# A decoder layer on one core: VectorE's order in the up-projection, and the pace of a gather's row fetches

## The chip, the cores and the metric

The kernel runs on one core of a Trainium2 chip. The metric is the device time of one execution in microseconds (us), lower being better. A core has five engines with an instruction queue each: TensorE (PE, with its weight loads as PEld), VectorE (DVE), ScalarE (ACT), GpSimd (POOL) and SyncE (SP), which here only issues transfers. ScalarE and GpSimd issue transfers too; all of them run on the core's 16 DMA engines.

## The reference

One decoder layer over 512 tokens of width 1024 in float32: token mixing (mLSTM heads and sliding-window attention), cross-attention into 256 memory tokens, then PEER, a retrieval over 128 x 128 single-neuron experts, and a final RMSNorm. The change lies in PEER, which per token is

```
qh = (xb @ w_pq).reshape(T, P_HEADS, 2, P_KEY_DIM)
v1, i1 = lax.top_k(s1, P_TOPK)          # s1, s2: scores against the two sets of 128 keys
v2, i2 = lax.top_k(s2, P_TOPK)
top_s, pos = lax.top_k(cand_s, P_TOPK)  # 16 of the 16 x 16 sums, for each of 8 heads
eidx = jnp.take_along_axis(cand_i, pos, axis=-1)
g = jax.nn.softmax(top_s, axis=-1)
u = expert_down[eidx]
a = jax.nn.gelu(jnp.einsum('thkd,td->thk', u, xb), approximate=False)
coef = g * a
out = jnp.einsum('thk,thkd->td', coef, expert_up[eidx])
```

So every token uses 8 x 16 = 128 experts, each with a row of 1024 in expert_down and one in expert_up.

## The kernel before

The 512 tokens are four blocks of 128 (NB = 4). PEER is done in two ways.

**Block 0 by gathering** (NG = 1). `gather` is a Python generator that issues one row step at a time. Step j < 128 fetches, for each of the 128 tokens, its j-th expert's row of expert_down (an indirect DMA on POOL's queue, 128 rows of 4 KB, into one of eight buffers "rows"), and VectorE multiplies it with the token and sums it into `dots` (L773). Then the coefficients are made, and steps 128 to 255 fetch rows of expert_up, which VectorE adds into `gacc` (L783). That is 256 row steps.

**Blocks 1 to 3 densely** (ND = 3, TD = 384 tokens). All 128 x 128 experts are treated as 128 tiles of 128 experts. A *down tile* (class `Down`) loads its weights in pairs (`draw`, GRP = 2), ScalarE casts them to dh, VectorE makes the remainder dl = draw − dh (L828), and TensorE computes 8 x 3 = 24 matmuls of 384 columns into acc_d (L839 to L841), which ScalarE puts through GELU. An *up tile* (`up_tile`) reads the gates `wt` of four tiles at a time from the DRAM tensor `wd`, the rows `uraw` of expert_up for two tiles at a time, and where the GELU output was spilled (72 of the tiles, SP) reads it back as `gsr`; VectorE multiplies it with the gates (cf, L898), ScalarE casts cf to ch and uraw to uh, VectorE makes the remainders cl (L901) and ul, called lo in the code (L891), and TensorE does 3 blocks x 2 halves x 3 = 18 matmuls of 512 columns into six PSUM banks acc_u (L912 to L914). uh, ul, ch and cl have two buffers each, so that the operands of tile u need those of tile u−2 to be done with.

**Stages around the change.** `gating` builds the dense gates of blocks 2 and 3 in 32 steps q each: one-hot tiles, eight matmuls per two groups into `w` (L745), ScalarE copies them to `stg` (two buffers), and after each eight steps a transfer of 2 MB writes stg to wd on ScalarE's queue. Between the steps, early down tiles fill TensorE. In block 3 the first 12 row steps of the gather are consumed at the steps q of GQ (9, 11, ... 31). Then come LEAD = 7 down tiles, the *lead*, with ten more row steps (GLD), and then the up-projection loop: 128 up tiles in the order of `up_order`, with the remaining 49 down tiles made ahead in it (`ahead`, `made_by`) and the remaining 256 − 22 row steps dealt out over tiles 0 to 119 (GST) by `rows`. The matmuls of the last two up tiles are ordered by block, so that `finish` (residual, final RMSNorm and the output) can begin by block; block 0 is finished from gacc.

**What sets the order.** The program is written in one order, and a planner (the Tile framework, with a timeline of its own) makes each engine's instruction order from the dependences and the written order as priority; the order on an engine is then fixed. `tc.issue_after(x)` keeps what is written in it behind x on x's own engine, in order of issue alone. In the loop before, VectorE's order is the planner's; each row step is only kept behind c.cf or c.cl of its tile. The row numbers come from `c.eidx`; row steps after the first 22 read a copy of it, `c.rowid`, which VectorE writes behind the last lead tile's dl (L1209).

Of the kernel before, what the change touches and what calls it, by code (L numbers as in the profile page):

```python
# [11 lines left out]
F32 = mybir.dt.float32  # L12
# [9 lines left out]
P = 128  # L22
# [29 lines left out]
GLD = 10  # L52
GST = 120
WST, WTL = 3, 5

# [643 lines left out]
def gating(c, early, ga):  # L699
# [3 lines left out]
    for b in range(NG + NS, NB):  # L703
# [29 lines left out]
        for q in range(32):  # L733
# [17 lines left out]
            with c.tc.issue_after(mm.ins):  # L751
                early.fill(FGT)
            if b == NB - 1 and q in GQ:
                with c.tc.issue_after(c.sc[HD - 1][-1].ins), c.tc.issue_after(last.ins):
                    step(ga, 1)


def gather(c):
# [6 lines left out]
    def fetch(src, j):  # L765
        r = gp.tile([P, D], F32, tag="rows", bufs=8, name="rows")
        G.indirect_dma_start(out=r, out_offset=None, in_=src,  # L767
                             in_offset=bass.IndirectOffsetOnAxis(ap=c.rowid[:, j:j + 1], axis=0))
        return r

    for j in range(P):
        r = fetch(c.a["down_r"], j)
        V.tensor_tensor_reduce(r, r, c.xn0, 1.0, 0.0, op0=ALU.mult, op1=ALU.add, accum_out=dots[:, j:j + 1])  # L773
        yield
# [3 lines left out]
    for j in range(P):  # L778
        r = fetch(c.a["up"], j)
        if j == 0:  # L780
            V.tensor_scalar(c.gacc, r, coef[:, j:j + 1], None, op0=ALU.mult)
        else:
            V.scalar_tensor_tensor(c.gacc, r, coef[:, j:j + 1], c.gacc, op0=ALU.mult, op1=ALU.add)  # L783
        yield


# [30 lines left out]
class Down:  # L817


    def __init__(self, c, i2):  # L820
        nc, dp = c.nc, c.dp
        self.c, self.i2 = c, i2
        if i2 % GRP == 0:
            c.draw = dp.tile([P, GRP, D], F32, tag="draw", bufs=2, name="draw")
            nc.sync.dma_start(c.draw, c.a["down_t"][i2 // GRP])
        raw = c.draw[:, i2 % GRP]
# [39 lines left out]

def up_tile(c, u, i2, gel, acc):
    nc, up = c.nc, c.up
    V, A, T = nc.vector, nc.scalar, nc.tensor
    if i2 % UG == 0:  # L870
        c.wt = up.tile([P, ND, UG * P], F32, tag="wt", bufs=2, name="wt")
        for b in range(ND):
            i = nc.sync.dma_start(c.wt[:, b], c.wd[b][i2 // UG])
            for j in c.sc[HD - 1] if b == 0 else ():
                c.tc.add_manual_dep(i.ins, j.ins.name, SYNC, reason="gates complete")
# [3 lines left out]
    if i2 % GRP == 0:  # L879
        c.uraw = up.tile([P, GRP, D], F32, tag="uraw", bufs=3, name="uraw")  # L880
        nc.sync.dma_start(c.uraw, c.a["up"].rearrange("(i p) d -> p i d", p=P)[:, i2:i2 + GRP])
    g = c.gsr[:, i2 % UG] if i2 < SP else gel[i2]
    raw = c.uraw[:, i2 % GRP]
    last = u == NK - 1
    if last:
        z = c.xlo.rearrange("p k t -> p (k t)")
        hi, lo = z[:, 0:D], z[:, D:2 * D]
        A.copy(hi, raw)
    else:
        hi, lo = split3(c, up, raw, "u", 2)  # L890
    V.tensor_tensor(lo, raw, f32(hi), op=ALU.subtract)  # L891
    cf = up.tile([P, TD], F32, tag="cf", bufs=2, name="cf")
    if last:
        ch, cl = z[:, 2 * D:2 * D + TD], z[:, 3 * D:3 * D + TD]
    else:
        ch = up.tile([P, TD], F32R, tag="ch", bufs=2, name="ch")
        cl = up.tile([P, TD], F32R, tag="cl", bufs=2, name="cl")
    c.cf = V.tensor_tensor(cf.rearrange("p (b t) -> p b t", t=32), g.rearrange("p (b t) -> p b t", t=32),  # L898
                    c.wt.rearrange("p b (q i t) -> p (b q) i t", q=4, i=UG)[:, :, i2 % UG], op=ALU.mult)
    A.copy(ch, cf)  # L900
    c.cl = V.tensor_tensor(cl, cf, f32(ch), op=ALU.subtract)  # L901
    return hi, lo, ch, cl
# [230 lines left out]
def body(tc, a, out, dbg=None):  # L1133
# [3 lines left out]
    with ExitStack() as st:  # L1137
# [57 lines left out]
        with pool("gather", side="right") as c.gp:  # L1195
            c.rowid = c.eidx
# [4 lines left out]
            assert len(gel) == SP  # L1201

            for n in range(LEAD):
                ahead(1)
                with tc.issue_after(c.dl.ins):
                    step(ga, GLD * (n + 1) // LEAD - GLD * n // LEAD)
            c.rowid = c.gp.tile([P, P], I32, name="rowid")
            with tc.issue_after(c.dl.ins):
                nc.vector.tensor_copy(c.rowid, c.eidx)  # L1209
            pst_ = [c.ps.tile([P, 512], F32, tag=t, name="acc_u") for t in "bbbbaa"]  # L1210
            acc = [[pst_[2 * b], pst_[2 * b + 1]] for b in range(ND)]
            last, mms = [], []
            g0 = len(GQ) + GLD
# [105 lines left out]
```

## Time and profile before

| | |
|---|---|
| median of 3 runs | 1648.53 us (1648.18 to 1648.61) |
| the profiled execution, its own time | 1650.35 us |
| its span, first to last instruction | 1648.7 us |
| TensorE busy | 1605.7 us (97%) |
| VectorE busy | 1233.7 us (75%) |
| ScalarE busy | 723.2 us (44%) |
| GpSimd busy | 590.8 us (36%) |

Times in the rows are us from the start of the span unless ns is named. Matmuls overlap in TensorE's pipeline and their ends are modelled, so the sum of their durations is more than the time from one start to the next. L912 is line 912 of the kernel before.

### The profile page before, as it was taken

To read this page: it belongs to the slowest core of one execution; us is meant where nothing else is said; L and a number is where in the kernel's file an instruction comes from. 1 tells how busy PE (TensorE), PEld (TensorE's weight loads), DVE (VectorE), ACT (ScalarE), POOL (GpSimd) and SP (SyncE) were. 2 spreads that over 40 slices of the span, in tenths; PEclk is the share of its full clock that TensorE was granted. 3 is DMA by queue.
4 is the path that set the end of the run, shared out by engine and by line. 5 is a ranking of instruction groups with operands and counts; after the bars stand their busy time and mean duration, and the time that the engine had idled before them with its cause. 6 is when DMAs were issued, how large, how long until landed. Compare 5 with 4: busy or idle time off the path is not lost.

```text
span 1648.7 us, 23081 instructions
## 1 busy us (share of the span) xinstructions
PE 1605.7 (97%) x8387; PEld 1411.7 (86%) x8388; DVE 1233.7 (75%) x2704; ACT 723.2 (44%) x1217; POOL 590.8 (36%) x427
## 2 busy tenths in 40 slices
PE   8998999999999999999999999999999999999994
PEld 5775698888999999999998888888888888888883
DVE  5366564564877887777787888787888888878898
ACT  5464444443544444578664333333333333333332
POOL 2000000000027787878121543443433444333451
PEclk9999999999999999999999999999999999999997
DMA  5227144232254435668999999999989999988895
GB/s 214 77 97 287 54 151 154 77 153 106 97 187 126 116 75 138 196 178 234 321 312 342 410 391 346 344 338 339 345 320 366 339 327 333 359 319 313 328 364 180
DMA packets 151122, 402.17 MB, mean 244 GB/s; under 512 B 28368, under 2 KB 62304, under 8 KB 138848
## 3 DMA queue, kind: packets, MB, share of 16 engines
q1 hardware_dynamic: 58208, 240.04, 39.4%
q0 software_dynamic: 55360, 134.32, 24.8%
q10 hardware_dynamic: 37440, 26.35, 5.1%
q8 instruction: 66, 1.08, 0.3%
q14 instruction: 48, 0.39, 0.1%
HBM read 357.07 MB, written 43.58 MB: 243 GB/s over the span
## 4 chain that ended last, share of the span: by engine, by line
PE 89%; DVE 4%; DMA 3%; ACT 1%; issue 1%; POOL 0%; DVEq 0%; SPq 0%; POOLq 0%; ACTq 0%
PE acc_u L912 10%; PE acc_u L913 10%; PE acc_u L914 10%; PE acc_d L841 10%; PE acc_d L839 10%; PE acc_d L840 10%; PE acc_f L1013 4%; PE acc_f L1015 4%; PE acc_f L1014 4%; PE w L745 3%; DMA wd<-stg 3%; PE acc_t L1026 2%; PE acc_t L1028 2%; PE acc_t L1027 2%; DVE gacc L783 1%
## 5 line engine op out<-in xcount | busy, mean ns | idle before, releaser
L839 PE MATMUL acc_d<-xhi,dh 128*128 128x384 f32 x1024 | 349.9, 342 | 1.1 <-ACT gsp L861 1.0
L841 PE MATMUL acc_d<-xhi,dl 128*128 128x384 f32 x1024 | 345.1, 337 | 1.7 <-DVE dl L828 1.7
L840 PE MATMUL acc_d<-xlo,dh 128*128 128x384 f32 x1024 | 343.7, 336 | 0.0
L913 PE MATMUL acc_u<-ul,ch 128*128 128x512 f32 x762 | 297.8, 391 | 0.0
L914 PE MATMUL acc_u<-uh,cl 128*128 128x512 f32 x762 | 296.7, 391 | 0.0
L690 POOL DMA_INDIRECT wd<-gg,ei x128 | 229.9, 1796 | 147.4 <-DVE ei L684 84.8
L912 PE MATMUL acc_u<-uh,ch 128*128 128x512 f32 x762 | 264.4, 390 | 0.1
L767 POOL DMA_INDIRECT rows<-in_up_dram,rowid x128 | 169.2, 1322 | 236.9 <-DVE gacc L783 209.0
L828 DVE TENSOR_TENSOR dl<-draw,dh 128x1024 fp32r<-128x1024 f32 x128 | 156.1, 1220 | 93.2 <-ACT dh L790 93.1
L900 ACT CAST ch<-cf 128x384 fp32r<-128x384 f32 x127 | 65.1, 514 | 356.6 <-issue 339.4
L790 ACT CAST dh<-draw 128x1024 fp32r<-128x1024 f32 x128 | 134.0, 1049 | 195.3 <-PE acc_d L840 179.4
L767 POOL DMA_INDIRECT rows<-in_down_r_dram,rowid x106 | 142.5, 1344 | 199.4 <-DVE dots L773 159.2
L839 PEld LDWEIGHTS acc_d<-xhi,dh 128*128 128x128 f32 x1024 | 192.9, 188 | 5.5 <-ACT gsp L861 1.3
L840 PEld LDWEIGHTS acc_d<-xlo,dh 128*128 128x128 f32 x1024 | 192.9, 188 | 3.7
L841 PEld LDWEIGHTS acc_d<-xhi,dl 128*128 128x128 f32 x1024 | 192.7, 188 | 4.0 <-DVE dl L828 2.6
L914 PEld LDWEIGHTS acc_u<-uh,cl 128*128 128x128 f32 x762 | 143.0, 188 | 29.4
L913 PEld LDWEIGHTS acc_u<-ul,ch 128*128 128x128 f32 x762 | 143.0, 188 | 28.7
L912 PEld LDWEIGHTS acc_u<-uh,ch 128*128 128x128 f32 x762 | 142.9, 188 | 28.3 <-ACT ch L900 0.5
L891 DVE TENSOR_TENSOR ul<-uraw,uh 128x1024 fp32r<-128x1024 f32 x127 | 154.8, 1220 | 12.4 <-ACT uh L790 11.9
L783 DVE SCALAR_TENSOR_TENSOR gacc<-rows,coef,gacc 128x1024 f32<-128x1024 f32 x127 | 162.6, 1280 | 0.9
L773 DVE CUSTOM_DVE_ANT_0 rows<-rows,xn 128x1024 f32<-128x1024 f32 x128 | 153.7, 1218 | 0.0
L901 DVE TENSOR_TENSOR cl<-cf,ch 128x384 fp32r<-128x384 f32 x127 | 70.7, 557 | 86.6 <-ACT ch L900 86.2
(344 smaller groups left out, 2644.7 us busy)
## 6 DMA issues: line engine op xcount, KB each, us to landing
draw<-in_down_t_dram SPq DMA_DIRECT2D x64, 1024.0 KB, 6.6
uraw<-in_up_dram SPq DMA_DIRECT2D x64, 1024.0 KB, 9.0
wt<-wd SPq DMA_DIRECT2D x96, 256.0 KB, 9.7
wd<-stg ACTq DMA_DIRECT2D x8, 2048.0 KB, 17.4
gd<-gsp SPq DMA_DIRECT2D x18, 768.0 KB, 3.9
gsr<-gd SPq DMA_DIRECT2D x18, 768.0 KB, 9.9
wd<-zero ACTq DMA_DIRECT2D x1, 8192.0 KB, 26.9
raw<-in_w_pq_dram SPq DMA_DIRECT2D x8, 1024.0 KB, 4.9
```

Of the source, the lines that this page charges most:

```text
L690: i = G.indirect_dma_start(out=out, out_offset=bass.IndirectOffsetOnAxis(ap=ei[:, h, k:k + 1], axis=0), in_=c.gg[:, NG, hh, k:k + 1], in_o ...
L767: G.indirect_dma_start(out=r, out_offset=None, in_=src, in_offset=bass.IndirectOffsetOnAxis(ap=c.rowid[:, j:j + 1], axis=0))
L773: V.tensor_tensor_reduce(r, r, c.xn0, 1.0, 0.0, op0=ALU.mult, op1=ALU.add, accum_out=dots[:, j:j + 1])
L783: V.scalar_tensor_tensor(c.gacc, r, coef[:, j:j + 1], c.gacc, op0=ALU.mult, op1=ALU.add)
L828: c.dl = nc.vector.tensor_tensor(self.lo, raw, f32(self.hi), op=ALU.subtract)
L839: T.matmul(acc[:, :TD], self.hi[:, ks], c.xhi[:, k, NG * P:], start=(k == 0), stop=False)
L840: T.matmul(acc[:, :TD], self.hi[:, ks], c.xlo[:, k, NG * P:], start=False, stop=False)
L841: T.matmul(acc[:, :TD], self.lo[:, ks], c.xhi[:, k, NG * P:], start=False, stop=(k == KT - 1))
L891: V.tensor_tensor(lo, raw, f32(hi), op=ALU.subtract)
L912: T.matmul(acc[b][n], ch[:, t], hi[:, d], start=st, stop=False)
L913: T.matmul(acc[b][n], ch[:, t], lo[:, d], start=False, stop=False)
L914: c.mm = T.matmul(acc[b][n], cl[:, t], hi[:, d], start=False, stop=sp)
```

## The change

Four things are changed, all in PEER.

1. From the first up tile to the last row step VectorE's instructions keep the written order (`tc.manual_schedule` for VectorE alone). The written order of a step u is now: half of the step's rows (rounded up), then lo and cl of tile u, the dl of down tiles made in the step, the other rows, and cf of tile u+1. For this `up_tile` is split: `up_gates` does the loads and cf one tile ahead.
2. The row numbers of the first 22 row steps are copied column by column into `c.rid` by VectorE (`row_number`), at every odd step q of the last gating block and once in each lead tile; a fetch reads its column there.
3. The copy of all row numbers, `c.rowid`, moves from behind the seventh lead tile to the fifth.
4. Gate reads (wt) and up loads (uraw) are kept behind the last lead tile's load (`c.lead`) on SyncE's queue.

```
+GI = range(1, 32, 2)
...
+            if b == NB - 1 and q in GI:
+                with c.tc.issue_after(last.ins):
+                    row_number(c)
...
         G.indirect_dma_start(out=r, out_offset=None, in_=src,
-                             in_offset=bass.IndirectOffsetOnAxis(ap=c.rowid[:, j:j + 1], axis=0))
+                             in_offset=bass.IndirectOffsetOnAxis(
+                                 ap=(c.rid if src is c.a["down_r"] and j < len(GQ) + GLD else c.rowid)[:, j:j + 1], axis=0))
...
+def row_number(c):
+
+    n = c.nid
+    if n < len(GQ) + GLD:
+        c.nc.vector.tensor_copy(c.rid[:, n:n + 1], c.eidx[:, n:n + 1])
+        c.nid += 1
...
-def up_tile(c, u, i2, gel, acc):
+def up_gates(c, u, i2, gel):
+
     nc, up = c.nc, c.up
-    V, A, T = nc.vector, nc.scalar, nc.tensor
     if i2 % UG == 0:
         c.wt = up.tile([P, ND, UG * P], F32, tag="wt", bufs=2, name="wt")
         for b in range(ND):
-            i = nc.sync.dma_start(c.wt[:, b], c.wd[b][i2 // UG])
+            with c.tc.issue_after(c.lead.ins):
+                i = nc.sync.dma_start(c.wt[:, b], c.wd[b][i2 // UG])
...
     if i2 % GRP == 0:
         c.uraw = up.tile([P, GRP, D], F32, tag="uraw", bufs=3, name="uraw")
-        nc.sync.dma_start(c.uraw, c.a["up"].rearrange("(i p) d -> p i d", p=P)[:, i2:i2 + GRP])
+        with c.tc.issue_after(c.lead.ins):
+            nc.sync.dma_start(c.uraw, c.a["up"].rearrange("(i p) d -> p i d", p=P)[:, i2:i2 + GRP])
     g = c.gsr[:, i2 % UG] if i2 < SP else gel[i2]
...
+    c.raw = c.uraw[:, i2 % GRP]
+    c.gated = up.tile([P, TD], F32, tag="cf", bufs=2, name="cf")
+    nc.vector.tensor_tensor(c.gated.rearrange("p (b t) -> p b t", t=32), g.rearrange("p (b t) -> p b t", t=32),
+                            c.wt.rearrange("p b (q i t) -> p (b q) i t", q=4, i=UG)[:, :, i2 % UG], op=ALU.mult)
+
+
+def up_tile(c, u):
...
+    V.tensor_tensor(lo, raw, f32(hi), op=ALU.subtract)
     A.copy(ch, cf)
-    c.cl = V.tensor_tensor(cl, cf, f32(ch), op=ALU.subtract)
+    V.tensor_tensor(cl, cf, f32(ch), op=ALU.subtract)
     return hi, lo, ch, cl
...
             for n in range(LEAD):
                 ahead(1)
                 with tc.issue_after(c.dl.ins):
+                    row_number(c)
+                    if n == LEAD - 3:
+                        c.rowid = c.gp.tile([P, P], I32, name="rowid")
+                        nc.vector.tensor_copy(c.rowid, c.eidx)
                     step(ga, GLD * (n + 1) // LEAD - GLD * n // LEAD)
-            c.rowid = c.gp.tile([P, P], I32, name="rowid")
-            with tc.issue_after(c.dl.ins):
-                nc.vector.tensor_copy(c.rowid, c.eidx)
+            assert c.nid == g0
+            c.lead = c.draw_dma
...
-            for u, i2 in enumerate(up_order()):
+            order = up_order()
+            dve = ExitStack()
+            dve.enter_context(tc.manual_schedule(engines={mybir.EngineType.DVE}))
+            up_gates(c, 0, order[0], gel)
+            for u, i2 in enumerate(order):
+                n = rows[u + 1] - rows[u]
+                step(ga, n - n // 2)
+                parts = up_tile(c, u)
                 if u >= FREE:
                     with tc.issue_after(mms[u - FREE].ins):
                         ahead(made_by(u) - len(gel))
                 else:
                     ahead(made_by(u) - len(gel))
-                parts = up_tile(c, u, i2, gel, acc)
-                for i in range(rows[u + 1] - rows[u]):
-                    with tc.issue_after((c.cf if i == 0 else c.cl).ins):
-                        step(ga, 1)
+                step(ga, n // 2)
+                if u < NK - 1:
+                    up_gates(c, u + 1, order[u + 1], gel)
...
             step(ga, 2 * P)
+            dve.close()
```

## Rows read from the trace of the kernel before

**Rows 1.** The page: span, and busy time of each engine.

```profile
span 1648.7 us, 23081 instructions
...
PE 1605.7 (97%) x8387; PEld 1411.7 (86%) x8388; DVE 1233.7 (75%) x2704; ACT 723.2 (44%) x1217; POOL 590.8 (36%) x427
```

**Rows 2.** The chain that ended last, from 1606 us: start, length, work.

```profile
1606.84 1.36 PE acc_u L912 x6
...
1610.92 1.33 PE acc_u L912 x6
...
1636.61 0.58 POOL frst L943
...
1642.42 1.32 DVE hb L931 x2
```

**Rows 3.** Stretches: length; each engine's busy time, instructions; granted clock; DMA share; GB/s.

```profile
892.00:1000.00 108.00, 108.00 (x521) 95.02 (x522) 89.05 (x132) 39.02 (x54) 49.61 (x38) 1.00 1.01 395
...
1620.00:1628.00 8.00, 7.24 (x32) 5.64 (x31) 7.86 (x7) 0.00 (x0) 0.76 (x1) 1.00 0.89 303
1628.00:1649.00 21.00, 0.00 (x0) 0.00 (x0) 14.37 (x27) 5.12 (x16) 2.16 (x4) 0.53 0.33 128
```

**Rows 4.** VectorE by line, 892 to 1627: count, busy us, mean ns, idle before.

```profile
L783 DVE SCALAR_TENSOR_TENSOR gacc<-rows,coef,gacc 128x1024 f32<-128x1024 f32 x124 | 158.7, 1280 | 0.8
L891 DVE TENSOR_TENSOR ul<-uraw,uh 128x1024 fp32r<-128x1024 f32 x126 | 153.7, 1219 | 10.9 <-ACT uh L790 10.3 <-DMA uraw<-in_up_dram 0.4
...
L901 DVE TENSOR_TENSOR cl<-cf,ch 128x384 fp32r<-128x384 f32 x127 | 70.7, 557 | 86.6 <-ACT ch L900 86.2
L828 DVE TENSOR_TENSOR dl<-draw,dh 128x1024 fp32r<-128x1024 f32 x50 | 61.1, 1222 | 24.2 <-ACT dh L790 24.2
```

**Rows 5.** Line L783 alone from 1594 us: count, ns min/median/max, starts.

```profile
L783 DVE SCALAR_TENSOR_TENSOR gacc<-rows,coef,gacc x18: 1271/1279/1285, 1593.1 to 1630.1; 128x1024 f32<-128x1024 f32 x18
```

**Rows 6.** Last gating block: stretches as in rows 3, ScalarE, gate writes' landing, POOL.

```profile
810.00:814.00 4.00, 1.89 (x13) 1.70 (x12) 2.58 (x7) 3.97 (x10) 0.00 (x0) 0.95 1.05 386
814.00:818.00 4.00, 4.00 (x20) 4.00 (x19) 2.89 (x8) 0.79 (x3) 1.15 (x1) 0.62 0.99 353
818.00:822.00 4.00, 4.00 (x29) 4.00 (x28) 2.60 (x8) 3.84 (x9) 0.00 (x0) 1.00 0.33 119
...
807.06 1.08 ACT L747 COPY stg<-w 128x512 f32<-128x512 f32 x2 [4.44 <-DMA wd<-stg]
...
DMA to landing us min/median/max: 12.2/17.4/27.0
...
774.71 1.13 POOL L767 DMA_INDIRECT rows<-in_down_r_dram,eidx  x1 [0.30 <-issue]
```

**Rows 7.** Final norm in order of time, VectorE and ScalarE.

```profile
1635.71 0.15 DVE L927 TENSOR_TENSOR frst<-fss 128x1 f32<-128x1 f32 x1
...
1635.78 0.68 DVE L925 TENSOR_TENSOR hb<-hb,acc_u 128x512 f32<-128x512 f32 x1
1635.85 0.58 ACT L926 ACTIVATE acc_u<-hb 128x512 f32<-128x512 f32 x1
```

**Rows 8.** ScalarE's casts for one up tile, in order of time.

```profile
1602.61 0.51 ACT L900 CAST ch<-cf 128x384 fp32r<-128x384 f32 x1 [2.61 <-issue]
1603.03 1.04 ACT L790 CAST uh<-uraw 128x1024 fp32r<-128x1024 f32 x1
```

**Rows 9.** Around the first up tile: SyncE, ScalarE, POOL, in order of time.

```profile
884.40 0.95 SPq L881 DMA_DIRECT2D uraw<-in_up_dram  x2
...
889.46 2.00 ACT L790 CAST uh<-uraw 128x1024 fp32r<-128x1024 f32 x2 [1.31 <-DMA uraw<-in_up_dram]
...
899.57 1.67 POOL L767 DMA_INDIRECT rows<-in_down_r_dram,rowid  x1 [26.81 <-DVE rowid L1209]
```

**Rows 10.** Row fetches, 900 to 930, then 1000 to 1600: median to landing.

```profile
rows<-in_down_r_dram,rowid POOLq DMA_INDIRECT x16, 14.6
...
rows<-in_down_r_dram,rowid POOLq DMA_INDIRECT x69, 7.2
```

More of the change, by code (lines that the diff above doesn't have):

```diff
@@ L772, in gather @@
         r = fetch(c.a["down_r"], j)
-        V.tensor_tensor_reduce(r, r, c.xn0, 1.0, 0.0, op0=ALU.mult, op1=ALU.add, accum_out=dots[:, j:j + 1])
+        c.row = V.tensor_tensor_reduce(r, r, c.xn0, 1.0, 0.0, op0=ALU.mult, op1=ALU.add, accum_out=dots[:, j:j + 1])
         yield
@@ L782, in gather @@
         else:
-            V.scalar_tensor_tensor(c.gacc, r, coef[:, j:j + 1], c.gacc, op0=ALU.mult, op1=ALU.add)
+            c.row = V.scalar_tensor_tensor(c.gacc, r, coef[:, j:j + 1], c.gacc, op0=ALU.mult, op1=ALU.add)
         yield
+def row_number(c):
[3 more added lines that the diff above has]
+        c.nid += 1
 def split3(c, pool, raw, tag, bufs):
@@ L824, in __init__ @@
             c.draw = dp.tile([P, GRP, D], F32, tag="draw", bufs=2, name="draw")
-            nc.sync.dma_start(c.draw, c.a["down_t"][i2 // GRP])
+            c.draw_dma = nc.sync.dma_start(c.draw, c.a["down_t"][i2 // GRP])
         raw = c.draw[:, i2 % GRP]
@@ L880, in up_tile @@
         c.uraw = up.tile([P, GRP, D], F32, tag="uraw", bufs=3, name="uraw")
-        nc.sync.dma_start(c.uraw, c.a["up"].rearrange("(i p) d -> p i d", p=P)[:, i2:i2 + GRP])
+        with c.tc.issue_after(c.lead.ins):
+            nc.sync.dma_start(c.uraw, c.a["up"].rearrange("(i p) d -> p i d", p=P)[:, i2:i2 + GRP])
     g = c.gsr[:, i2 % UG] if i2 < SP else gel[i2]
-    raw = c.uraw[:, i2 % GRP]
-    last = u == NK - 1
-    if last:
+    c.raw = c.uraw[:, i2 % GRP]
[3 more added lines that the diff above has]
+def up_tile(c, u):
+    nc, up = c.nc, c.up
+    V, A = nc.vector, nc.scalar
+    raw, cf = c.raw, c.gated
+    if u == NK - 1:
         z = c.xlo.rearrange("p k t -> p (k t)")
         hi, lo = z[:, 0:D], z[:, D:2 * D]
+        ch, cl = z[:, 2 * D:2 * D + TD], z[:, 3 * D:3 * D + TD]
         A.copy(hi, raw)
@@ L890, in up_tile @@
         hi, lo = split3(c, up, raw, "u", 2)
[L891 to L895, printed above, removed]
         ch = up.tile([P, TD], F32R, tag="ch", bufs=2, name="ch")
         cl = up.tile([P, TD], F32R, tag="cl", bufs=2, name="cl")
-    c.cf = V.tensor_tensor(cf.rearrange("p (b t) -> p b t", t=32), g.rearrange("p (b t) -> p b t", t=32),
-                    c.wt.rearrange("p b (q i t) -> p (b q) i t", q=4, i=UG)[:, :, i2 % UG], op=ALU.mult)
+    V.tensor_tensor(lo, raw, f32(hi), op=ALU.subtract)
     A.copy(ch, cf)
-    c.cl = V.tensor_tensor(cl, cf, f32(ch), op=ALU.subtract)
+    V.tensor_tensor(cl, cf, f32(ch), op=ALU.subtract)
     return hi, lo, ch, cl
@@ L1195, in body @@
         with pool("gather", side="right") as c.gp:
-            c.rowid = c.eidx
+            c.rid = c.gp.tile([P, len(GQ) + GLD], I32, name="rid")
+            c.nid = 0
             ga = gather(c)
@@ L1201, in body @@
             assert len(gel) == SP
+            g0 = len(GQ) + GLD
             for n in range(LEAD):
@@ L1212, in body @@
             last, mms = [], []
-            g0 = len(GQ) + GLD
             due = [WST * u + WTL * made_by(u) for u in range(-1, GST)]
```

## The prediction

> **What bounds the kernel now.** I read the page first, then the chain that ended last, stretches of the span, VectorE's groups, and then the places where TensorE starts fewer matmuls than usual. On the page TensorE is busy for 97% of the span [rows 1]. That alone says little, because the ends of matmuls are modelled; what counts is how regularly they start. In the up-projection the chain shows six matmuls of an up tile in 1.36 us and the next tile's six 4.08 us later [rows 2]: 18 matmuls at 0.227 us, no hole. From 892 to 1627.2 us TensorE does 128 up tiles and 50 down tiles [rows 3, 4] (the count of L828 is that of down tiles). 735.2 − 128 × 4.08 = 213 us for 50 down tiles is 4.26 us each, 0.178 us per matmul: there TensorE sets the pace and nothing I save on another engine shortens it.
>
> Two places are not like that.
>
> - The end. TensorE's last matmul is over at 1627.24 (7.24 us busy in the window from 1620, none after 1628) and the span goes on to 1648.7 [rows 1, 3]. The chain leaves TensorE as early as 1612.25 (1610.92 + 1.33) and ends with VectorE [rows 2]. Eighteen of the loop's 234 gathered rows (256 less the 22 taken before it) are accumulated between 1593.1 and 1630.1, the last 1.28 us ending about 1631.4 [rows 5]. The final norm starts behind them. That is 1648.7 − 1627.24 = **21.5 us** without a matmul.
> - The gating. Around 812 us TensorE starts 13 and then 20 matmuls in windows of 4 us in which 29 is usual, and the granted clock falls to the lower of its two levels, 1.2 of 2.4 GHz, for a part of them (0.62 as the mean of the second window) [rows 6]. The missing 25 starts are 25 × 4/29 = **3.4 us**. Backwards: ScalarE's copy to stg waited 4.44 us for a gate write; it ended at 807.06, so this is the slowest write, which landed after 27.0 us (issued about 780) where the median is 17.4; the gather's first eight row fetches are issued from 774.71 on, one behind the other, and stand in its way [rows 6].
>
> Besides, VectorE waits in the loop: 86.6 us for ch, 24.2 us for dh and 10.9 us for uh, 121.7 us in all [rows 4].
>
> **Part by part.**
>
> *VectorE in program order, rows in halves.* No tile operation is added or removed. A step of an up tile alone is then: one row, lo, cl, next cf: 1.28 + 1.22 + 0.56 + 0.56 (cf has cl's shape) = 3.6 us of 4.08; a down tile adds dl and two rows, 1.22 + 2 × 1.28 = 3.8 us of 4.26 [rows 4]. So the order fits with some 10% left. All rows then stand ahead of tile 120, whereas 18 of them were left for the last eight tiles. They are 18 × 1.28 = 23 us of VectorE; the cover is the 121.7 us in which it waits now. With cover gone they would stop TensorE for what is not hidden.
>
> After TensorE's end there remains one block: add 0.68, square 0.58, two small operations of 0.15, POOL 0.58, two scalings 1.32, then what follows the last scaling, 1648.7 − 1643.74 = 4.96 [rows 1, 2, 7]. Sum 8.4 us, without what lies between them; the block before can stand in front with its own scalings, up to 1.3 us. I take 9.1, bounds 8.4 and 9.9: a saving of **12.4 us**, bounds 11.6 to 13.1.
>
> What the order costs in the loop: lo(u) needs buffers that tile u−2 frees, and dl of the step's down tile now stands behind lo(u) and cl(u). From the end of u−2: ch and uh 1.46 us [rows 8], lo 1.22, cl 0.56, dl 1.22 [rows 4]: 4.46 us. TensorE wants dl after one up tile and two matmuls that need only dh: 4.08 + 0.36 = 4.44. That is level. From below 0, from above one cast of 1.04 us on each of the 50 down tiles, 52 us; 16 of a down tile's 24 matmuls don't read dl and can go first (16 × 0.178 = 2.8 us of cover), as the six of L912 do now [rows 2]. I take **+1.3**, near the lower end for that reason.
>
> The Trainium skill, PSUM — Partial Sum Buffer, Engine vs sequencer instructions, says the queues of ScalarE, VectorE and GpSimd are strictly first in, first out. The trace agrees for POOL: one waiting fetch held POOL for 26.81 us [rows 9]. By that rule alone each late row or dl would hold every operation behind it, which is the slower rival below; it changes its chance, not the sum.
>
> *Paced fetches.* Sixteen one-column copies on VectorE release a fetch each at every second step of the last gating block instead of eight at once, six more in the lead. Each copy is below 0.15 us (a 128x1 operation) [rows 7], 22 of them 3.3 us at most, under VectorE's waits; uncovered it would still not be TensorE's time. Without eight fetches of 512 KB in its way the gate write should land near the median 17.4 us, and ScalarE began to wait for it only at 802.6 (807.06 − 4.44), after some 22.6 us. Saving **3.4 us**, bounds 0 and 4.
>
> *Gate reads and up loads behind tile loads; row numbers two tiles sooner.* Now the first gate reads wait for the last gate write to land, and the first up loads come behind them at 884.40; ScalarE has the first up tile at 889.46 [rows 9]. In the new order one more tile load passes ahead, which feeds the seventh lead tile to TensorE before the first up tile instead of after. The gate write still has to land, so the loads behind it do not start sooner: gain 0. But POOL, held until 899.57 by the row numbers now [rows 9], gets them two down tiles (8.5 us) earlier, so that row fetches run beside the first gate reads and up loads, and in VectorE's order the first row stands ahead of lo(0). Rows land in 7.2 us (median, middle of the loop) but took 14.6 us in the crowded opening [rows 10]. With 7.2 us lo(0) is about on time; with 14.6 it is 7 us late, less the 1.36 us of L912 matmuls. So 0 to +6; I take **+2.5**, nearer the quiet value, as fewer fetches are waiting at once.
>
> The Trainium skill, DMA: Bandwidth & Descriptors, Anatomy of one DMA, gives 2.0 us plus bytes over 436 GB/s: for a row fetch of 512 KB an estimate of 3.2 us. The rows say 7.2 and 14.6, so the measurement decides; with the page's figure the +2.5 would be 0 and the forecast 2.5 us lower.
>
> **Sum.** −12.4 + 1.3 − 3.4 + 2.5 = −12.0 us. The profiled execution took 1650.35 us, 1.65 us around its span of 1648.7 and 1.8 us over the median of the runs, 1648.53; the differences are carried over to the median: **1636.5 us**.
>
> **Rivals.**
>
> *The down split comes late (slower).* The price is above: the break-even is (12.0 + 1.3)/50 = 0.27 us late per down tile. One cast or row of about 1 us ahead of dl on half of them is 25 us, giving 1661. For it: the level sum of 4.46 against 4.44, and waits for dh already there [rows 4]. Against it: those waits cost TensorE nothing now, and dh matmuls can go first. Chance 0.14.
>
> *The opening eats the gain of the gating.* The moved fetches slow the last gate write from 17.4 to 27.0 us: up loads 9.6 us later, of which the extra lead tile covers 4.26; 5.3 us of stop, plus 1.5 us for matmuls at half clock behind it, as at 814 us (4 us at 0.62 [rows 6]). That is 6.8 in place of the 2.5: 1641. With a late first row as well, some 1645. For it: the opening moves 395 GB/s with a DMA share of 1.01 [rows 3]. Against: the same number of bytes in all. Chance 0.14.
>
> *The order does not do what it says.* Late rows use up VectorE's waits, and the 23 us of rows stop TensorE earlier instead of lengthening the end. Then only the gating's 3.4 us less the opening's 2.5 are left: 1647.6, no change. Against: 7.2 us landing with eight buffers, eight rows being about 25 us of work. Chance 0.08.
>
> **Numbers.** The forecast's own case has the remaining 0.64 and reaches from 1631.4 (13.1 + 4.0 saved, nothing lost) to 1643 (11.6 saved, 6 lost in the opening). For 8 in 10 I go from 1628, since small stops in the lead for which I count no gain could go too, up to 1648, the unchanged time nearly; that leaves out the slower rival and a little on each side. A measurement can tell about 0.2%, 3.3 us. Faster by more: 0.64 and most of the opening's 0.14 with a remnant of the last case, 0.80; within: 0.06; slower: 0.14.
>
> **What would show it.** Right: 18 rows gone from after the last eight tiles; TensorE's last matmul some 9 us before the end; matmul starts of 29 per 4 us throughout the last gating block, with gate writes under 22 us; row fetches one by one through it instead of eight in a row. Wrong: idle on TensorE ahead of L841 with dl as releaser, repeated at every down tile; a gap ahead of the first L913 with ul as releaser; a granted clock of half inside the loop; waits of VectorE for rows. If the end is short but the time is not, the loss is to be looked for between 865 and 900 and then in the loop's rate per tile.

## The result: slower by 0.8%, and the profile after

The changed kernel, called after below, takes 1661.62 us (median of four runs, 1659.30 to 1663.32) against 1648.53 before: a ratio of 1.0076, 95% interval 1.0064 to 1.0089. The prediction was 1636.5. The profiled execution took 1659.3 us with a span of 1657.5, the fastest of its four, so the two traces explain +8.8 us of span and not the whole +13.1 of the medians.

One measure runs through what follows. An undisturbed down matmul starts 0.1735 us after the last one, an up matmul 0.2277 us. A stretch less its matmuls times these two figures is what TensorE lost in it. All 3,072 down and 2,304 up matmuls are in the traces. The rows up to 930 also hold TensorE's other work, as many matmuls in both kernels (505 from 700 to 860), so there only the difference counts.

| us | before | after | difference | predicted |
|---|---|---|---|---|
| lost before 700 | | | +0.3 | 0 |
| lost 700 to 860 (gating) | 60.6 | 56.9 | -3.7 | -3.4 |
| lost 860 to 930 (opening of the up-projection) | 4.4 | 25.0 | **+20.6** | +2.5 |
| lost 930 to 1600 (loop) | 2.3 | 1.6 | -0.7 | +1.3 |
| lost from 1600 to TensorE's last matmul | 0.1 | 0.9 | +0.8 | 0 |
| last matmul to the end | 21.4 | 12.9 | -8.5 | -12.4 |
| sum, against the span | 1648.7 | 1657.5 | +8.8 (+8.8) | -12.0 |

The gating gains what was forecast, the end two thirds of it, and the loop costs nothing; the opening, forecast at +2.5, outweighs them. The page of after, against [rows 1]; TensorE's busy share is 97% as before, which shows once more how little it says:

```profile
span 1657.5 us, 23008 instructions
...
PE 1609.5 (97%) x8387; PEld 1412.5 (85%) x8388; DVE 1225.5 (74%) x2726; ACT 727.6 (44%) x1217; POOL 627.1 (38%) x427
```

The stretches of after, against [rows 3] (length, busy time of each engine, granted clock, DMA share, GB/s). From 892 to 930 TensorE is busy for 23.12 of 38 us, at a granted clock of 0.78 in the mean; behind it nothing is missing:

```profile
892.00:930.00 38.00, 23.12 (x91) 19.03 (x91) 19.57 (x31) 6.92 (x10) 16.37 (x13) 0.78 0.93 362
930.00:1300.00 370.00, 370.00 (x1776) 324.50 (x1776) 306.48 (x437) 134.43 (x183) 171.50 (x125) 1.00 0.94 358
...
1620.00:1658.00 38.00, 24.62 (x109) 20.07 (x107) 18.66 (x32) 11.02 (x22) 1.62 (x3) 0.86 0.11 42
```

TensorE in order of time in that stretch (start, length, work, in brackets the idle time before it and what ended it). The first two up tiles are 36 matmuls, 8.2 us of work; they take from 894.25 to 921.98. There are two stops, 3.47 and 11.41 us, and after each of them six matmuls take 2.2 to 2.9 us in place of 1.36, because the clock is granted at half, 1.2 of 2.4 GHz ("issue" names no releaser; VectorE's rows below show it):

```profile
894.25 1.55 PE L933 MATMUL acc_u<-uh,ch 128*128 128x512 f32 x6
899.27 2.19 PE L934 MATMUL acc_u<-ul,ch 128*128 128x512 f32 x6 [3.47 <-issue]
901.25 2.62 PE L935 MATMUL acc_u<-uh,cl 128*128 128x512 f32 x6
915.28 2.93 PE L933 MATMUL acc_u<-uh,ch 128*128 128x512 f32 x6 [11.41 <-ACT ch L921]
918.01 2.76 PE L934 MATMUL acc_u<-ul,ch 128*128 128x512 f32 x6
```

ScalarE over the same time. It is in time with the first two casts uh; then the cast dh of a down tile of step 80/81 waits 18.35 us for its load, and ch of the second up tile, a cast of 0.51 us whose cf is ready at 900.2, stands behind it for the last 13.6 of these:

```profile
893.04 2.00 ACT L805 CAST uh<-uraw 128x1024 fp32r<-128x1024 f32 x2 [1.42 <-DMA uraw<-in_up_dram]
...
913.77 1.04 ACT L805 CAST dh<-draw 128x1024 fp32r<-128x1024 f32 x1 [18.35 <-DMA draw<-in_down_t_dram]
914.72 0.51 ACT L921 CAST ch<-cf 128x384 fp32r<-128x384 f32 x1
```

VectorE, in its fixed order: the row ahead of lo(0) is late by 4.04 us, which makes the smaller stop, and cl of the second tile waits 12.83 us for that ch:

```profile
896.84 1.23 DVE L780 CUSTOM_DVE_ANT_0 rows<-rows,xn 128x1024 f32<-128x1024 f32 x1 [4.04 <-DMA rows<-in_down_r_dram,rowid]
...
915.26 0.56 DVE L922 TENSOR_TENSOR cl<-cf,ch 128x384 fp32r<-128x384 f32 x1 [12.83 <-ACT ch L921]
```

SP's queue, against [rows 9]: the first gate reads hold it for 13.12 us until the gate write has landed, the up loads follow at 886.72, and the load for which ScalarE waits goes out at 889.77 and lands about 24 us later:

```profile
873.55 13.12 SPq L889 DMA_DIRECT2D wt<-wd  x3
886.72 0.95 SPq L898 DMA_DIRECT2D uraw<-in_up_dram  x2
...
889.77 0.43 SPq L840 DMA_DIRECT2D draw<-in_down_t_dram  x1
```

What else is under way: from 885 to 905 us the queue of the row fetches (q0, POOL's) moves as many bytes as SP's (q1); packets, MB, share of the 16 engines' time, and the issues of POOL:

```profile
q1 hardware_dynamic: 1235, 3.60, 47.4%
q0 software_dynamic: 1022, 3.73, 47.3%
...
rows<-in_down_r_dram,rowid POOLq DMA_INDIRECT x10
```

Before, POOL stood until 899.57 [rows 9], and the same 20 us belonged to SP:

```profile
q1 hardware_dynamic: 2185, 7.79, 99.9%
q0 software_dynamic: 31, 0.13, 1.6%
```

The bytes asked for account for a wait of this size. From 886.7 us on the DMA engines are asked for three up loads (3 MB), six gate reads (1.5 MB), the tile load (1 MB) and ten row fetches (5 MB): 10.5 MB of 1024 KB, at this stretch's 369 GB/s some 30 us. That estimate is on the high side; eight of the ten rows go out after the tile load. Without the rows it is 5.5 MB and 15.6 us.

One more thing holds the up loads back. Before, the last gate write went out at 866.6 and landed 17.4 us later. In after it went out 3.2 us sooner, at 863.4, but the gate read that waits for it left SP only at 886.35, up to 22.9 us later. So the lead ends sooner and the first up load is issued 2.3 us later (886.72 for 884.40).

The gating, against [rows 6]: no hole and no half clock in the last block, and ScalarE's copies to stg wait for TensorE alone, no longer for a gate write:

```profile
810.00:814.00 4.00, 4.00 (x31) 4.00 (x29) 4.00 (x12) 2.26 (x6) 1.43 (x1) 1.00 1.13 377
814.00:818.00 4.00, 4.00 (x28) 4.00 (x28) 3.04 (x11) 3.76 (x9) 0.77 (x2) 1.00 1.04 421
```

VectorE by line from 922 to 1645, against [rows 4]: dl never waits, ch is waited for less (35.5 us for 86.2), uh more (83.1 for 10.3), and TensorE loses nothing by it:

```profile
L920 DVE TENSOR_TENSOR ul<-uraw,uh 128x1024 fp32r<-128x1024 f32 x124 | 151.5, 1221 | 83.3 <-ACT uh L805 83.1
...
L922 DVE TENSOR_TENSOR cl<-cf,ch 128x384 fp32r<-128x384 f32 x124 | 68.5, 553 | 35.6 <-ACT ch L921 35.5
L843 DVE TENSOR_TENSOR dl<-draw,dh 128x1024 fp32r<-128x1024 f32 x48 | 58.5, 1219 | 0.0
```

The end, against [rows 5, 7]: the last gathered row is accumulated at 1605.7 instead of 1630.1. VectorE then makes five final adds in a row, the first at 1642.17 after a wait for TensorE, whose last matmul ends at 1644.62; a sixth add and the scalings follow, and 5.7 us after the last of them the span ends:

```profile
1642.17 3.08 DVE L946 TENSOR_TENSOR hb<-hb,acc_u 128x512 f32<-128x512 f32 x5 [4.85 <-PE acc_u L935]
...
1646.64 2.74 DVE L952 SCALAR_TENSOR_TENSOR hb<-hb,frst,xn 128x512 f32<-128x512 f32 x4 [0.41 <-POOL frst L964]
...
1650.37 1.42 DVE L952 SCALAR_TENSOR_TENSOR hb<-hb,frst,xn 128x512 f32<-128x512 f32 x2 [0.73 <-POOL frst L964]
```

The 0.8 us lost after 1600 are one stop. With its rows done early, block 0 has its final norm in the middle of the up tiles, and its two scalings stand ahead of a tile's ul on VectorE:

```profile
1610.44 1.41 DVE L952 SCALAR_TENSOR_TENSOR hb<-hb,frst,xn 128x512 f32<-128x512 f32 x2 [0.69 <-POOL frst L964]
...
1611.78 1.22 DVE L920 TENSOR_TENSOR ul<-uraw,uh 128x1024 fp32r<-128x1024 f32 x1
...
1613.05 1.65 PE L934 MATMUL acc_u<-ul,ch 128*128 128x512 f32 x6 [0.61 <-DVE ul L920]
```

### The profile page after: what moved, and what is told of

Its sections match the earlier page's. It is cut to its first block, busy times and chain, and to the rows that moved or that the text cites. A ratio compares the mean times of both kernels' runs of the same rounds, so it can differ in the third digit from the quotient of the medians.

```text
span 1657.5 us, 23008 instructions
## 1 busy us (share of the span) xinstructions
PE 1609.5 (97%) x8387; PEld 1412.5 (85%) x8388; DVE 1225.5 (74%) x2726; ACT 727.6 (44%) x1217; POOL 627.1 (38%) x427
## 4 chain that ended last, share of the span: by engine, by line
PE 90%; DVE 3%; DMA 3%; ACT 1%; issue 1%; POOL 0%; SPq 0%; POOLq 0%; DVEq 0%; ACTq 0%
PE acc_u L934 10%; PE acc_u L933 10%; PE acc_u L935 10%; PE acc_d L856 10%; PE acc_d L855 10%; PE acc_d L854 10%; PE acc_f L1034 4%; PE acc_f L1036 4%; PE acc_f L1035 4%; PE w L748 3%; PE acc_t L1047 2%; PE acc_t L1048 2%; PE acc_t L1049 2%; DMA draw<-in_down_t_dram 1%; DMA wd<-stg 1%
## 5 line engine op out<-in xcount | busy, mean ns | idle before, releaser
L773 POOL DMA_INDIRECT rows<-in_up_dram,rowid x128 | 194.6, 1520 | 184.0 <-DVE gacc L790 160.7
L805 ACT CAST uh<-uraw 128x1024 fp32r<-128x1024 f32 x127 | 133.5, 1052 | 251.5 <-PE acc_u L935 184.5
L933 PE MATMUL acc_u<-uh,ch 128*128 128x512 f32 x762 | 216.0, 393 | 11.4 <-ACT ch L921 11.4
L934 PE MATMUL acc_u<-ul,ch 128*128 128x512 f32 x762 | 220.8, 393 | 4.1 <-issue 3.5
L935 PE MATMUL acc_u<-uh,cl 128*128 128x512 f32 x762 | 219.1, 391 | 0.0
L920 DVE TENSOR_TENSOR ul<-uraw,uh 128x1024 fp32r<-128x1024 f32 x127 | 155.1, 1221 | 83.3 <-ACT uh L805 83.1
L1022 DVE TENSOR_TENSOR wlo<-raw,whi 128x2048 fp32r<-128x2048 f32 (+3 forms) x51 | 86.4, 1708 | 43.8 <-ACT whi L1021 43.8
```

What stands on the lines that cost most here:

```text
L773: G.indirect_dma_start(out=r, out_offset=None, in_=src, in_offset=bass.IndirectOffsetOnAxis(ap=(c.rid if src is c.a["down_r"] and j < len( ...
L805: c.nc.scalar.copy(hi, raw)
L933: T.matmul(acc[b][n], ch[:, t], hi[:, d], start=st, stop=False)
L934: T.matmul(acc[b][n], ch[:, t], lo[:, d], start=False, stop=False)
L935: c.mm = T.matmul(acc[b][n], cl[:, t], hi[:, d], start=False, stop=sp)
```

## The experiments

Theory A: the row fetches, let go two down tiles sooner, crowd out the tile load. B: the load's place on SP's queue is at fault. C: it is ScalarE's order, a cast that waits for a load ahead of one that doesn't. Each of the ten kernels was timed against the kernel before in the same session. "Loss" is TensorE's from 860 to 930 us, 4.4 before and 25.0 after.

**Row numbers behind the second up tile, no rows in the first up tiles** (tests A; all the rest as after)

```diff
-                    if n == LEAD - 3:
-                        c.rowid = c.gp.tile([P, P], I32, name="rowid")
-                        nc.vector.tensor_copy(c.rowid, c.eidx)
...
-            rows = [(2 * P - g0) * (d - due[0]) // (due[-1] - due[0]) for d in due]
+            rows = [(2 * P - g0) * max(0, d - due[4]) // (due[-1] - due[4]) for d in due]
...
                 parts = up_tile(c, u)
+                if u == 1:
+                    nc.vector.tensor_copy(c.rowid, c.eidx)
```

> The changed kernel, but VectorE copies the row numbers of the later fetches only behind cl of up tile 1, and the steps 0 to 3 of the loop have no rows (the same rows are dealt out over steps 4 to 119). SyncE's order is the same as in the changed kernel. Theory A (the ten row fetches that POOL issues from 887 to 902 crowd out the load of down tile 80, which lands after about 24 us and holds ScalarE's queue): the load lands in 12 us or less, ScalarE's longest wait for it falls from 18.4 us to under 6, TensorE's stop of 11.4 us goes or falls under 4; about 1646 us, 15 us less than the changed kernel. Theory B (the load is late by its place on SyncE's queue, behind gate reads and three up loads): no change, 1658 to 1663 us, the wait stays over 14 us.

Measured: 1641.74 us, ratio to before 0.9953 [0.9937, 0.9970]. Loss 9.6. The tile load lands after 14.0 us (A gave 12 or less) and no cast waits for it. But the planner has given ScalarE another order too: dh of tile 80 now stands behind ch of the first four up tiles, where in after it stood ahead of the second's. So this run takes away A and C together. What is left is one stop of 3.51 us for the first cast uh, whose load went out at 889.44:

```profile
896.75 1.99 ACT L805 CAST uh<-uraw 128x1024 fp32r<-128x1024 f32 x2 [3.47 <-DMA uraw<-in_up_dram]
...
909.38 1.05 ACT L805 CAST dh<-draw 128x1024 fp32r<-128x1024 f32 x1
```

The row queue's share of the DMA engines from 885 to 905 us is 14.9% in place of 47.3%:

```profile
q1 hardware_dynamic: 1679, 5.71, 75.0%
q0 software_dynamic: 291, 1.05, 14.9%
```

**The load of down tiles 80 and 81 ahead of the gate reads** (tests B)

```diff
-            c.lead = c.draw_dma
+            k = SP + LEAD + 1
+            c.draw_next = c.dp.tile([P, GRP, D], F32, tag="draw", bufs=2, name="draw")
+            c.lead = nc.sync.dma_start(c.draw_next, c.a["down_t"][k // GRP])
```

(and the step of tiles 80 and 81 takes this tile instead of loading one)

> The changed kernel, but the load of down tiles 80 and 81 is put ahead of the first gate reads on SyncE's queue, so that the gate reads and up loads stand behind it. The row fetches are as in the changed kernel. Theory A (row fetches crowd it out): it is issued some 5 us sooner, before most of the fetches, and lands by about 897; the up loads, now last, are late instead by 2 to 6 us; about 1648 to 1652 us. Theory B (place on the queue): the load lands in 9 us, nothing else is late, about 1642 us.

Measured: 1647.31 us, ratio 0.9991 [0.9982, 1.0001], nearer A's 1648 to 1652 than B's 1642. Loss 12.0. No cast dh waits any more, and the stop moves to the first cast uh (6.14 us of TensorE), whose load now lands late in the same crowd.

**The casts of a step's down tiles behind its ch on ScalarE** (tests C)

```diff
-    A.copy(ch, cf)
+    c.ch = A.copy(ch, cf)
...
+                with tc.issue_after(c.ch.ins):
+                    if u >= FREE:
+                        with tc.issue_after(mms[u - FREE].ins):
+                            ahead(made_by(u) - len(gel))
...
```

> The changed kernel, but in the loop ScalarE's casts for a step's down tiles stand behind its cast ch of the same step's up tile. Theory C (the price comes from ScalarE's order: the cast that waits for the late load stands ahead of ch of tile 1): up tiles 1 and 2 run while the load is on its way; VectorE then waits at dl of tile 80, so TensorE stops some 5 to 8 us instead of 19.5 in the opening; 1648 to 1651 us. Rival (every order waits for the load alike): 1658 to 1663 us.

Measured: 1644.68 us, ratio 0.9978 [0.9965, 0.9991], below the 1648 to 1651 expected. Loss 14.4 in the trace, which is of a run of 1649.77 (the seven lie between 1642.85 and 1649.77); a stop of 7.44 us for the first cast uh. The tile load lands as late as ever, 26.3 us after its issue at 892.9, and hurts nobody. The same load in the first experiment, issued at 893.9, took 14.0:

```profile
draw<-in_down_t_dram SPq DMA_DIRECT2D x1, 1024.0 KB, 26.3
```

So no one of A, B and C makes the stop of 11.41 us alone: with the row numbers held, with the load moved ahead or with the casts moved behind ch, it is gone. Of the 19.9 us that the first experiment gives back between the medians, ScalarE's order by itself gives 16.9. What the row fetches cost with this order mended is measured by the last two experiments.

**The paced fetches alone, on the kernel before**

```diff
+            if b == NB - 1 and q in GI:
+                with c.tc.issue_after(last.ins):
+                    row_number(c)
...
-                             in_offset=bass.IndirectOffsetOnAxis(ap=c.rowid[:, j:j + 1], axis=0))
+                             in_offset=bass.IndirectOffsetOnAxis(
+                                 ap=(c.rid if src is c.a["down_r"] and j < len(GQ) + GLD else c.rowid)[:, j:j + 1], axis=0))
...
```

> The kernel before with the paced fetches alone (row numbers copied column by column in the last gating block and in the lead). Theory: the stop of TensorE at 812 us goes, the slowest gate write lands in under 22 us, 3.4 us less: 1645 us (1644 to 1646). Rival (the six fetches moved into the lead slow the last gate write and eat the gain): 1648 us or more.

Measured: 1658.10 us, ratio 1.0054 [1.0038, 1.0071]. Up to 860 us it loses 56.9, so the 3.7 us of the gating are the pacing's own. They are not kept: TensorE is done with the lead sooner and waits 4.43 us for the first cast uh, since the gate write still holds SP's queue (17.23 us here; the write takes 21.0 us to land, 17.4 before), as the rival had it, and the planner now leaves 26.0 us after the last matmul in place of 21.4.

```profile
892.30 1.22 PE L924 MATMUL acc_u<-uh,ch 128*128 128x512 f32 x2 [4.43 <-ACT uh L802]
```

**After without the reordered loads** (the fourth part of the change undone: gate reads and up loads free of the tile loads)

```diff
-            with c.tc.issue_after(c.lead.ins):
-                i = nc.sync.dma_start(c.wt[:, b], c.wd[b][i2 // UG])
+            i = nc.sync.dma_start(c.wt[:, b], c.wd[b][i2 // UG])
...
-        with c.tc.issue_after(c.lead.ins):
+        if True:
             nc.sync.dma_start(c.uraw,
```

> The changed kernel without its third part: gate reads and up loads no longer stand behind the tile loads on SP's queue; rows, row numbers and VectorE's order as in the changed kernel. Theory (late tile load in a crowd of row fetches, held to by ScalarE in order): the loads of two down-tile pairs now stand behind the first gate reads and go out with the ten row fetches, so casts dh wait for both and ch stands behind them: the stretch 892 to 930 loses as much as in the changed kernel or more, 18 to 35 us in place of 19.7, and the time is 1658 to 1675. Rival (the moved loads themselves delay the first gate reads and up loads, and so the first up tiles): the loss goes to below 5 us and the time to 1642 to 1648.

Measured: 1654.62 us, ratio 1.0034 [1.0021, 1.0047]; loss 21.0, of it 13.8 after 892 us. That is less than the theory gave (18 to 35) and far more than the rival did (below 5). The moved loads are thus not the whole cause, but they make it worse, by 7.0 of the 13.1 us between the medians and by 4.0 us of loss in the traces. There are two stops of 5.96 and 5.79 us, one for an up load, one for the tile loads:

```profile
894.42 1.99 ACT L805 CAST uh<-uraw 128x1024 fp32r<-128x1024 f32 x2 [4.97 <-DMA uraw<-in_up_dram]
...
903.14 1.99 ACT L805 CAST dh<-draw 128x1024 fp32r<-128x1024 f32 x2 [6.34 <-DMA draw<-in_down_t_dram]
```

**After without VectorE's program order**

```diff
-            dve.enter_context(tc.manual_schedule(engines={mybir.EngineType.DVE}))
```

> The changed kernel without VectorE's program order: the planner orders VectorE again, fetches, row numbers and loads as changed. Theory: the crowd of row fetches is still there and the tile load of 80 and 81 still lands late (over 20 us), but only ch of tile 3 stands behind its cast now, so the stretch 892 to 930 loses 4 to 14 us in place of 19.7; rows are back at the end, so 20 to 26 us follow TensorE's last matmul in place of 12.9; together 1650 to 1661. Rival one (VectorE's fixed order, a late row ahead of lo, is what cost the opening): the loss goes to below 2 us and with the long end the time is 1645 to 1649. Rival two (the order does not shorten the end): 13 us follow the last matmul as in the changed kernel.

Measured: 1659.55 us, ratio 1.0060 [1.0042, 1.0078]. Loss 12.1 in place of 25.0, and 26.0 us after the last matmul in place of 12.9. So the order is what shortens the end, by 13.1 us against this version, and it loses 12.9 us in the opening: what it gained at the one place it gave away at the other. The tile load is late here too (10.67 us of waiting on ScalarE), but only the fourth tile's ch is behind it:

```profile
913.36 1.04 ACT L805 CAST dh<-draw 128x1024 fp32r<-128x1024 f32 x1 [10.67 <-DMA draw<-in_down_t_dram]
```

and 25 rows are accumulated from 1590.4 us on, where after has seven from 1579.7:

```profile
L790 DVE SCALAR_TENSOR_TENSOR gacc<-rows,coef,gacc x25: 1276/1280/1285, 1590.4 to 1640.5; 128x1024 f32<-128x1024 f32 x25
```

**Held row numbers, and the last two up tiles written block by block** (for the end)

```diff
                 for n in range(2):
-                    for i, u in enumerate(last):
-                        up_mm(c, NK - 2 + i, u, acc, b, (n,))
+                    with tc.issue_after(c.mm.ins):
+                        for i, u in enumerate(last):
+                            up_mm(c, NK - 2 + i, u, acc, b, (n,))
```

> The version with the row numbers behind the second up tile (1641.7 us), and the last two up tiles' matmuls written out block by block and half by half, so that a block's sum is complete before the next one's begins. Theory (the planner put all of tile 126 ahead of all of tile 127, so that six final adds come due together): the time between TensorE's last matmul and the end goes from 12.9 to between 8.5 and 10.5 us, and the time to 1637.5 to 1639.5. Rival (12.9 us are what the last block's own chain of add, square, scaling and store needs): 12.5 to 13.5 us and 1641 to 1643.

Measured: 1640.47 us, ratio 0.9951 [0.9933, 0.9969]: against the 1641.74 of the version it is built on that is less than the runs differ among themselves. The trace tells more: 11.05 us after the last matmul in place of 12.87, between the two expectations. The adds come one by one now, but the last block's two small operations, with its squares done at 1626.55, still stand behind another block's scaling on VectorE:

```profile
1625.11 0.69 DVE L946 TENSOR_TENSOR hb<-hb,acc_u 128x512 f32<-128x512 f32 x1
...
1626.59 1.41 DVE L952 SCALAR_TENSOR_TENSOR hb<-hb,frst,xn 128x512 f32<-128x512 f32 x2 [0.73 <-POOL frst L964]
1627.92 0.15 DVE L948 TENSOR_TENSOR frst<-fss 128x1 f32<-128x1 f32 x1
...
1628.99 1.42 DVE L952 SCALAR_TENSOR_TENSOR hb<-hb,frst,xn 128x512 f32<-128x512 f32 x2 [0.73 <-POOL frst L964]
```

In the profiled execution (1637.82 us) there is no stop after 892 (loss 6.5, all of it before):

```profile
892.00:930.00 38.00, 38.00 (x184) 33.28 (x183) 30.90 (x46) 15.79 (x22) 19.50 (x16) 1.00 1.03 410
```

**The same, and the first up loads ahead of the first gate reads**

```diff
-            with c.tc.issue_after(c.lead.ins):
-                i = nc.sync.dma_start(c.wt[:, b], c.wd[b][i2 // UG])
+            with c.tc.issue_after(c.ul.ins):
+                i = nc.sync.dma_start(c.wt[:, b], c.wd[b][i2 // UG])
```

(the block that issues the up load stands ahead of the one that reads the gates, and its instruction is c.ul)

> As the one before, and the first up loads ahead of the first gate reads on SP's queue, where the gate reads wait for the last gate write. Theory (what is left of the opening's loss, 5.5 us, is SP held by the gate reads while up loads that do not depend on the gates stand behind them): the first cast uh no longer waits, the stretch 892 to 930 loses 0 to 2.5 us, the time is 1633 to 1636. Rival (the up loads then fill the DMA engines while the last gate write lands, so that gate reads and cf come later by what uh gains): loss 4 to 8 us, 1638 to 1641.

Measured: 1639.56 us, ratio 0.9945 [0.9927, 0.9963]; loss 6.9, of it 1.6 after 892 us. That stretch is inside the theory's 0 to 2.5, but the time is the rival's, and nothing is gained over the version before it. The first up load goes out at 873.85, but the gate reads hold SP until 891.1 now and ch waits for cf, as the rival had it:

```profile
895.83 0.51 ACT L921 CAST ch<-cf 128x384 fp32r<-128x384 f32 x1 [2.96 <-DVE cf L902]
```

**Held rows, but row numbers back in the lead** (after with this one line; the crowd by itself: VectorE uses no row before the fifth up tile, and ScalarE's order in the opening is that of the first experiment)

```diff
-            rows = [(2 * P - g0) * (d - due[0]) // (due[-1] - due[0]) for d in due]
+            rows = [(2 * P - g0) * max(0, d - due[4]) // (due[-1] - due[4]) for d in due]
```

> The version with held row numbers (1641.7 us), but with the row numbers back in the lead, where the changed kernel has them: ten rows are fetched from about 887 us on as in the changed kernel, yet VectorE uses none of them before the fifth up tile, and ScalarE's order in the opening is that of the held version. Theory (the bytes of the row fetches make tile and up loads late): the load of down tiles 80 and 81 takes over 20 us to land in place of 14, up loads over 12 in place of 9, the stretch from 860 to 930 loses 12 to 20 us in place of 9.6, and the time is 1644 to 1652. Rival (late rows ahead of lo in VectorE's fixed order did it): loss and time as in the held version, 8 to 10.5 us and 1640 to 1643.

Measured: 1647.05 us, ratio 0.9978 [0.9966, 0.9990]; loss 14.1. Time and loss are the theory's, but two of its marks are not: the tile load's cast starts at 912.41 without waiting, so it landed after at most 19.8 us, and the first up load, issued at 888.5, after 10.2 us, which is 2.9 more than in the first experiment (7.3). TensorE stops for 2.31 and 4.52 us. The row queue has 52.7% of the DMA engines from 885 to 905 us:

```profile
q0 software_dynamic: 1084, 3.92, 52.7%
q1 hardware_dynamic: 1120, 3.21, 42.3%
```

It is a smaller crowd than the expectation says: since VectorE frees no buffer, only six of the ten rows go out by 892, and the seventh waits until 912.75:

```profile
891.99 0.94 POOL L773 DMA_INDIRECT rows<-in_down_r_dram,rowid  x1 [0.30 <-issue]
912.75 1.68 POOL L773 DMA_INDIRECT rows<-in_down_r_dram,rowid  x1 [19.82 <-DVE dots L780]
```

Six rows make 8.5 MB in place of 10.5, by the same estimate 24 us, where the tile load took 19.8 at most.

**The same fetches with a sixteenth of the bytes** (for row numbers 22 to 31, 64 columns in place of 1024; VectorE reads them 15 times over)

```diff
+        few = src is c.a["down_r"] and 22 <= j < 32
-        G.indirect_dma_start(out=r, out_offset=None, in_=src,
+        G.indirect_dma_start(out=r[:, :64] if few else r, out_offset=None, in_=src.rearrange("n (k d) -> (n k) d", d=64) if few else src,
...
```

> As the one before, but the ten rows fetched in the opening (numbers 22 to 31) are cut to their first 64 of 1024 columns (32 KB in place of 512 KB a fetch), and VectorE reads those 64 columns 15 times over, so that its work stays about the same; the ten dot products are then others. Theory (bytes): tile load below 16 us, loss from 860 to 930 back to 6 to 10.5 us, time 1638 to 1643. Rival (the number of fetches and packets, or POOL's queue itself, not the bytes): load over 20 us and a time as in the version before, whatever that was.

Measured: 1639.42 us, ratio 0.9950 [0.9932, 0.9968]; loss 5.4. The tile load lands 13.5 us after its issue at 891.5, and the stop for the first cast uh is 1.39 us:

```profile
893.45 2.00 ACT L808 CAST uh<-uraw 128x1024 fp32r<-128x1024 f32 x2 [0.96 <-DMA uraw<-in_up_dram]
...
905.03 1.05 ACT L808 CAST dh<-draw 128x1024 fp32r<-128x1024 f32 x1 [0.47 <-DMA draw<-in_down_t_dram]
```

Six fetches at the same times in POOL's queue, and 7.6 us less between the medians. So it is not the number of fetches. Bytes and packets are not told apart, since the packets of POOL's queue from 885 to 905 us fell too, from 1084 to 435:

```profile
q0 software_dynamic: 435, 1.06, 17.3%
```

## Why the prediction was wrong

**The step that failed is the opening: +2.5 us, bounds 0 and 6; it measured +20.6.** The prediction saw that the row numbers would come two down tiles sooner and that row fetches would then run beside the first gate reads and up loads. It priced this as one thing only, a late first row ahead of lo(0), and there it was right: that stop is 3.47 us, inside the bounds. Three things it did not price.

- It took "fewer fetches are waiting at once" for granted. Ten went out between 887.3 and 901.6, 5 MB where the whole stretch needs 5.5 MB of up, gate and tile loads. That the bytes in all are the same, which stood there against the second rival, is true and beside the point: they came together with the loads that TensorE needed next. With ScalarE's order mended, the bulk of six of these rows is worth 8.7 us of loss (14.1 with full rows, 5.4 with thin ones), or 4.5 against rows that are held (9.6).
- It did not follow ScalarE's order. The planner put dh of 80/81 ahead of ch of the second up tile. With the load late that is another 10.6 us (25.0 in after, 14.4 with the casts behind ch), the larger part. VectorE's fixed order brought it along: where the planner orders VectorE, dh stands behind ch of the third up tile and the opening loses 12.1. The strict first-in-first-out queues of the Trainium skill, PSUM — Partial Sum Buffer, Engine vs sequencer instructions, were cited for VectorE and POOL; here the trace agrees for ScalarE, which stood 18.35 us at a waiting cast, the last 13.6 of them with a ready one behind it.
- It did not price the clock in this term: around both stops the granted clock was half, 1.2 of 2.4 GHz; the 18 up matmuls behind the second took 6.7 us (915.28 to 921.98) in place of 4.1.

For loads that pile up, durations read from a quiet stretch don't hold. The Trainium skill, DMA: Bandwidth & Descriptors, Anatomy of one DMA, has its sum for a transfer that GpSimd issues; carried over to SP's tile load of 1 MB it would give an estimate of 4.4 us (2.0 us and 1 MB over 436 GB/s). The measurement differs and decides. The tile load took 13.5 to 14.0 us with the rows held or thin and 24 to 26.3 us with ten of them. Bytes asked for over GB/s moved, 15.6 and 30 us, is the better estimate of the two, and on the high side.

**The end: −12.4, measured −8.5; the mechanism was right, the size off.** The rows are gone from the end, and undoing the order alone brings them back (26.0 us). But 9.1 us after the last matmul assumed that only one block, or a block and a bit, is left there. In after six of eight final adds fall due within 3.7 us, since the last tile's matmuls all come after the one before. Writing them by block gives 11.05. Of the 1.95 left to 9.1, some 0.7 is what follows the last scaling (5.7 us for 4.96) and the rest, as the rows of that version suggest but no run tests, VectorE's order.

**The gating: −3.4, measured −3.7.** Right, and shown by the pacing alone. What the prediction missed is that a lead which ends sooner needs its up loads sooner, while the last gate write lands no sooner: by itself the pacing makes the kernel slower.

**The order in the loop: +1.3, measured −0.7.** Right that it costs next to nothing there; dl waits nowhere from 922 on. The slower rival gave 1661, which is the measured time by luck: its mechanism is not there, as no down tile in the loop stops TensorE. The second rival was nearest, as it had the opening eat the gating's gain, but it looked for the harm in the gate write alone and priced it at 6.8. The write was slower (up to 22.9 us for 17.4; it gave 27.0), and so the sign of under 22 us failed for it, but the two stops are not its work: the first up load was in time for the first up tile.

What stays open: the 2.3 us between the profiled run of after and its median, which no trace here covers; how the moved loads bring in their 7 us; and whether it is the rows' bytes or their packets that delay the other loads.

The experiments lead to a version that beats both kernels: after with the row numbers held back, and with the last two tiles by block and the first up loads ahead, 1639.56 us (ratio 0.9945). The hold alone, 1641.74, is most of it; the intervals of the two overlap, so that the other two edits gain anything is not shown.

## What to carry to other kernels

When an edit frees a queue sooner, list what it will issue from that moment, add up the bytes, and divide by the GB/s of that stretch: that time is an estimate, here on the high side, of when whatever is issued behind it lands. Then look on each in-order engine for a ready instruction behind one that waits for such a load. Prefetches that nobody needs yet should be released after the loads that open a stage, not with them.

## What the runs showed of the hardware

From 885 to 905 us, with both queues full, the DMA engines gave POOL's row fetches about half of their time (47.3%, and 47.4% to SP, in after; 52.7% and 42.3% with the crowd alone; 60.8% and 34.8% with the casts behind ch), although SP had the loads that mattered. The same load of 1 MB, issued between 891.5 and 893.9, took 13.5 us with thin rows, 14.0 with rows held and 26.3 with ten full rows. And a stop of 3.5 us on TensorE was already followed by a granted clock of half, in after from 900.16 to 903.58.
